# Two chained transformer layers on one core: the end of the expert stage and the start of the second block are re-ordered

## The chip, the cores and the metric

The kernel runs on one core of a Trainium2 chip. The metric is the device time of one execution in microseconds (us), the median of several runs; less is better. TensorE (PE) multiplies matrices, VectorE (DVE) and ScalarE (ACT) do elementwise work, GpSimd (POOL) issues the indirect gathers, SyncE (SP) issues the other transfers.

## The reference

Two blocks are chained, on 512 tokens of width 1024. What matters here is the seam between them:

```
# end of block 1
f = peer_ffn(hn2, ...)              # expert mixture: sum over picked experts of gelu(h.u[e]) * gate * v[e]
x = x + gate2 * f
x = rmsnorm(x, final_g)             # output of block 1
# start of block 2
h  = concat([16 meta tokens, x])    # 528 rows
n1 = rmsnorm(h, norm1_w)
q, k, v, fg, u = split(n1 @ w_in)   # k is normed per head
mix = concat([forgetting_attention(q, k, v, cumsum(log_sigmoid(fg))), pooled_means(u) @ w_pool]) @ w_out
h = h + mix                         # then a gated feed-forward layer; the meta rows are dropped at the end
```

## The kernel before, in words

Activations lie transposed (width on the partitions), 128 tokens to a tile, four tiles. A float32 product is made of three PE passes over a high and a low part (`mm3`, L189 to L191). Weights come by DMA as float32 chunks (`raw`), and `split_chunk` (L176 to L185) makes of each the pair `whi` (an ACT copy, L183) and `wlo` (a DVE subtraction, L184). Both parts lie in rings of a few slots that are taken in turn (`ring`, L107 to L117); a chunk's slot is that of the chunk some places earlier, so its copy waits until the last matmul on that earlier chunk is done. While `open_raw` is in force the ring has extra slots behind the base ones.

Each engine works through its own list of instructions in order. The order of a list is set when the program is built, by a scheduler that weighs the written order, its own costs for each instruction and readiness; `issue_after` ties an instruction behind another.

*Expert stage.* Three of the four token tiles ("dense" tiles) are multiplied with all expert rows: 128 chunks, each a 128x1024 slice of `v`, accumulate in six PSUM banks `a`, two for each tile. The fourth tile (`GB`) instead gathers its picked rows one by one (POOL indirect DMA into `grow`, DVE L1056 adds each into `gacc`). `GFUSE` and `GTAIL` set how many gathers are written beside each chunk and how many chunks before the end the last one stands. The last three chunks (`VT`) are written apart, tile by tile.

*Finisher* (`fin`, L1165 to L1187), once for each tile: z = f times gate2 (L1169 for GB, L1174 for a dense tile, in two halves read from PSUM), x += z (L1170 or L1175), a row sum of squares on ACT (L283), x *= final_g (L1177), a second row sum, two reciprocal roots by small 128x1 operations (L267 to L275; their root on ACT), the norm rows z = x * r2 * w1 (L1184), PE transposes and a split of these into `nh`, `nl` (L249, L256, L257), and x *= r1 (L1186, the output of block 1 itself). `z` has one of two slots `fz`. `meta_norm` (L1189) does the 16 meta rows.

*Key stage.* `k2_proj` (L1201) splits the four key weight chunks, then `go` projects the keys of a tile in two halves of the width (`part` 0 and 1), and `headnorm` norms them per head (`hq`, `hss`, `ks`). `KORD` is the order: small letters are first halves, capitals second halves (m meta, g GB, a, b, c the dense tiles), f the finisher of the last dense tile. Then come the q projection (`q_fill`), the forget gate features (PE into a 72-row tile, added on DVE at L1301), values, and eight attention heads with other work filled between them (`B2F`).

*End of block 2's mixing.* `mix_fill` (L1420) multiplies the pooled half of the width with its part of `w_out`, and adds to x in L1431, on 128x512. The attention half is `gemm_rows` on `w_out` (L1479) in four chunks, whose ring has extra slots from `open_raw` at L1460, after the attention pool is closed.

Of the kernel before, what the change touches and what calls it, by code (L numbers as in the profile page):

```python
# [11 lines left out]
F32 = mybir.dt.float32  # L12
F32R = mybir.dt.float32r
# [11 lines left out]
D = 1024  # L25
KC = 8
# [25 lines left out]
LAG = 6  # L52
CB = 4
GBB = 2
GFUSE = 2.75
GTAIL = 6
GLAG = 3
NGAT = 257 + GLAG
VT = 3
# [6 lines left out]
WPF = ('', '', 'a', '', 'ra', 'ra', 'ra', 'r')  # L66
ADKB = 3
TG = 4
KORD = 'amfbgcMAGBC'
B2F = ('', 'b', 'af', 'q', 'ec', 'dg', 'vijkh', 'lCAB', 'DW', 'XY', 'Z')  # L70
CANDS = ((0, 1, 16, 0), (1, 4, 8, 16), (4, 8, 4, 40), (8, 16, 1, 56))
GSC = 16384.0
# [3 lines left out]
class Kern:  # L76
# [73 lines left out]
    def consts(self):  # L150
        nc, I, cp = self.nc, self.I, self.cp
        self.table()
        cst = cp.tile([128, 5, 128], F32, name="cst")
        nc.sync.dma_start(cst, I["cst"].rearrange("c p n -> p c n"))
        self.ident = cst[:, 0]
        self.cneg = cst[:, 3]
        self.identb = cp.tile([128, 128], BF, name="identb")
        nc.vector.tensor_copy(self.identb, cst[:, 0])
        self.ntri = cp.tile([128, 128], F32R, name="ntri")
        nc.vector.tensor_copy(self.ntri, cst[:, 1])  # L160
        self.nones = cp.tile([128, 128], F32R, name="nones")
        nc.vector.memset(self.nones.bitcast(F32), -1.0)
        self.onesf = cp.tile([128, 128], F32, name="onesf")
        nc.vector.memset(self.onesf, 1.0)
        self.strictT = cp.tile([128, 128], BF, name="strictT")
        nc.vector.tensor_copy(self.strictT, cst[:, 2])
        self.cposb = cp.tile([128, 128], BF, name="cposb")
        nc.vector.tensor_scalar(self.cposb, cst[:, 3], -1.0, None, op0=ALU.mult)
        self.iota = cst[:, 4]
        self.epsc = cp.tile([128, 1], F32, name="epsc")  # L170
        nc.vector.memset(self.epsc, EPS)
        self.cols2 = cp.tile([128, 6], F32, name="cols2")
        self.iota_h = cp.tile([128, 128], HF, name="iota_h")
        nc.vector.tensor_copy(self.iota_h, cst[:, 4])

    def split_chunk(self, src):  # L176
        nc = self.nc
        shp = [128] + list(src.shape[1:])
        raw = self.row(shp)
        self.loaded = nc.sync.dma_start(raw, src).ins  # L180
        hi = self.ring(shp, F32R, "whi")
        lo = self.ring(shp, F32R, "wlo")
        nc.scalar.activation(hi, raw, AF.Copy)  # L183
        self.lastlo = nc.vector.tensor_tensor(lo, raw, hi, op=ALU.subtract).ins  # L184
        return hi, lo  # L185
# [74 lines left out]
            r = nc.vector.scalar_tensor_tensor(lo, src, scale, hi, op0=ALU.mult, op1=ALU.subtract)  # L260
        return r.ins

    def rstd(self, pool, ssum, n, cols, rows=128, eps=None):
        nc = self.nc
        h, r, q = [pool.tile([128, cols], F32, name=self.nm("r" + c))[:rows] for c in "hrq"]
        e, eh = (self.epsc[:, 0:1], -0.5 * EPS) if eps is None else eps
        nc.vector.tensor_scalar(h, ssum, -0.5 / n, eh, op0=ALU.mult, op1=ALU.add)  # L267
        nc.scalar.activation(r, ssum, AF.Ln, scale=1.0 / n, bias=e[:rows])
        nc.scalar.activation(r, r, AF.Exp, scale=-0.5)
        if cols == 1:  # L270
            nc.vector.scalar_tensor_tensor(q, h, r, r, op0=ALU.mult, op1=ALU.mult)
        else:
            nc.vector.tensor_tensor(q, r, r, op=ALU.mult)
            nc.vector.tensor_tensor(q, q, h, op=ALU.mult)
        nc.vector.scalar_tensor_tensor(r, q, 1.5, r, op0=ALU.add, op1=ALU.mult)  # L275
        return r

    def sumsq(self, pool, src, n, rows=128):
        nc = self.nc
# [715 lines left out]
    def peer(self):  # L995
# [138 lines left out]
        self.ks = pa.tile([128, 2, 4, W1], F32R, name="ks")  # L1134
        kctx = ExitStack()
        pn = kctx.enter_context(tc.tile_pool(name="b2k", bufs=1))
        tgen = self.v_chunk(pv, accs, tail)
        next(tgen)
        kproj = self.k2_proj(pn)
        fin(dense[0], accs[0])  # L1140
        fin(dense[next(tgen)], accs[1])
        next(tgen)
        for c in KORD:
            if c == "f":
                fin(dense[2], accs[2])
            else:
                t = (-1, GB, *dense)["mgabcMGABC".index(c) % 5]
                kproj((t,), "mgabcMGABC".index(c) // 5)
# [5 lines left out]
    def finisher(self, pool):  # L1154
        nc, I = self.nc, self.I
        self.table()
        rows = {}
        for k, src in (("g2", self.modrow[3:4]), ("fg", I["final_g"]), ("w1", I["n1w"])):
            rows[k] = self.grows()
            with self.tc.issue_after(self.loaded):  # L1160
                self.brow(rows[k], src)
        self.n1w = rows["w1"]
        self.n1 = n1h, n1l = self.act_pair(W1)

        def fin(t, f):  # L1165
            x = self.x[:, t]
            z = pool.tile([128, D], F32, tag="fz", bufs=2, name=self.nm("fz"))
            if t == GB:
                nc.vector.tensor_tensor(z, f, rows["g2"], op=ALU.mult)  # L1169
                nc.vector.tensor_tensor(x, x, z, op=ALU.add)  # L1170
            else:
                for n in range(2):
                    c = ts(n, 512)
                    nc.vector.tensor_tensor(z[:, c], f[n], rows["g2"][:, c], op=ALU.mult)  # L1174
                    nc.vector.tensor_tensor(x[:, c], x[:, c], z[:, c], op=ALU.add)  # L1175
            s1 = self.sumsq(pool, x.unsqueeze(1), 1)
            nc.vector.tensor_tensor(x, x, rows["fg"], op=ALU.mult)  # L1177
            s2 = self.sumsq(pool, x.unsqueeze(1), 1)
            r1 = self.rstd(pool, s1, D, 1)
            e2 = pool.tile([128, 2], F32, name=self.nm("e2"))  # L1180
            nc.vector.tensor_scalar(e2[:, 0:1], s1, EPS / D, EPS * EPS, op0=ALU.mult, op1=ALU.add)
            nc.vector.tensor_scalar(e2[:, 1:2], s1, -0.5 * EPS / D, -0.5 * EPS * EPS, op0=ALU.mult, op1=ALU.add)
            r2 = self.rstd(pool, s2, D, 1, eps=(e2[:, 0:1], e2[:, 1:2]))
            nc.vector.scalar_tensor_tensor(z, x, r2, rows["w1"], op0=ALU.mult, op1=ALU.mult)  # L1184
            self.rows_out(n1h, n1l, META + 128 * t, z, None if t == GB else self.psa)
            nc.vector.tensor_scalar(x, x, r1, None, op0=ALU.mult)  # L1186
        return fin  # L1187

    def meta_norm(self, pool):  # L1189
        nc = self.nc  # L1190
        n1h, n1l = self.n1
        mt = pool.tile([128, D], F32, tag="fz", bufs=2, name="mt")[:META]
        nc.sync.dma_start(mt, self.I["meta"])
        rm = self.rstd(pool, self.sumsq(pool, mt.unsqueeze(1), 1, META), D, 1, META)
        nc.vector.scalar_tensor_tensor(mt, mt, rm, self.n1w[:META], op0=ALU.mult, op1=ALU.mult)
        p = self.psg()
        for k in range(KC):
            nc.tensor.transpose(p[:, ts(k, META)], mt[:, ts(k, 128)], self.ident[:META, :META])
        self.hilo(n1h[:, :, 0:META], n1l[:, :, 0:META], p[:, 0:KC * META].rearrange("p (k n) -> p k n", n=META))

    def k2_proj(self, pn):  # L1201
        tc, I = self.tc, self.I
        n1h, n1l = self.n1
        wv = I["w_in_2"].rearrange("(k p) n -> p k n", p=128)
        kwc = self.cols2[:, 1:2]
        ck = [self.split_chunk(wv[:, kc:kc + 2, 512:1024]) for kc in range(0, KC, 2)]

        ps = {}

        def go(ts_, part):  # L1210
            for t in ts_:
                c = slice(0, META) if t < 0 else slice(META + 128 * t, META + 128 * t + 128)
                m = META if t < 0 else 128
                if part != 1:
                    p = ps[t] = self.psg() if t in (-1, GB) else self.psa()
                    for k in range(KC):
                        hi, lo = ck[k // 2]
                        self.mm3(p[:m], n1h[:, k, c], n1l[:, k, c], hi[:, k % 2], lo[:, k % 2], k == 0, k == KC - 1)
                if part != 0:
                    self.headnorm(pn, ps[t], kwc, self.ks, c, m)  # L1220
        return go

    def headnorm(self, pool, p, wcol, dst, off, rows, half=None, q=None, ps=None):
        nc = self.nc
# [25 lines left out]
    def block2(self, out):  # L1250
# [170 lines left out]
        def mix_fill(g):  # L1421
            hi, lo = self.split_chunk(wov[:, 4:8, ts(g, 256)])
            for tp in (0, 2):
                p = self.psg()
                for k in range(4):
                    mh_, ml_ = mixed(4 + k)
                    for t in range(2):
                        c = ts(tp + t, 128)
                        self.mm3(p[:, ts(t, 256)], mh_[:, c], ml_[:, c], hi[:, k], lo[:, k], k == 0 and t == 0, k == 3, skip=True)
                xs = x[:, tp:tp + 2, ts(g, 256)]  # L1430
                nc.vector.tensor_tensor(xs, xs, p.rearrange("p (t n) -> p t n", n=256), op=ALU.add)  # L1431

        fill = {"q": lambda: q_fill(1), "v": lambda: v_fill(1)}
        for g in range(4):
# [182 lines left out]
```

## Time and profile before

| quantity | value |
|---|---|
| median of three runs | 2385.33 us (2384.72 to 2385.57) |
| profiled execution | 2384.28 us, span of its trace 2382.4 us |
| PE busy | 2302.8 us, 97% of the span |
| DVE, ACT, POOL busy | 73%, 43%, 14% |
| last expert matmul starts | 1752.36 us from the start of the span |

The time axis of every view starts at the start of the span. A row of the timeline is one instruction, or several alike in a row; the bracket at its end is the time that the engine had been idle before it, and who released it. PE rows overlap, since a matmul starts before the one ahead of it has drained: the distance between two starts is what one costs.

### The profile page before, as it was taken

Reading aid. Unit: us, or ns where it says so; the run is one execution under the profiler, and the core shown is the slowest. Engines: PE = TensorE matmul, PEld = TensorE weight load, DVE = VectorE, ACT = ScalarE, POOL = GpSimd, SP = SyncE. Lnnn points to the kernel's source line nnn. Section 1 sums busy time; section 2 is a strip of 40 time slices with the busy share of each in tenths; the row PEclk is TensorE's granted clock in tenths of the full one; section 3 lists DMA queues with packets and bytes.
Section 4 is the critical chain, followed back from the end, with each engine's and each line's share of the span. In section 5 each row is a group of like instructions: output and inputs, shape, how many; then the busy total and the mean of one; then the engine's idle time right before and its main releaser. Section 6 shows DMA issues by size and latency. Waiting matters only on the chain.

```text
span 2382.4 us, 33726 instructions
## 1 busy us (share of the span) xinstructions
PE 2302.8 (97%) x12405; PEld 2013.1 (85%) x12409; DVE 1744.0 (73%) x3421; ACT 1030.3 (43%) x1642; POOL 326.3 (14%) x286
## 2 busy tenths in 40 slices
PE   7999888999999999999999999999989989999999
PEld 6888766778899999999999988888868878888887
DVE  7689876677998998876888898888886765333321
ACT  3587444243355665553333333333345543322211
POOL 0000000000000323432344432222200000000000
PEclk9999999999999999999999999999989989999999
DMA  9432644652255999989999999999943312333231
GB/s 268 116 98 63 187 141 132 207 165 80 87 179 165 349 357 352 340 337 331 313 334 340 339 376 358 334 338 348 343 136 91 102 36 80 107 97 97 90 116 43
DMA packets 282217, 498.63 MB, mean 209 GB/s; under 512 B 19442, under 2 KB 176754, under 8 KB 280516
## 3 DMA queue, kind: packets, MB, share of 16 engines
q1 hardware_dynamic: 243268, 355.96, 44.8%
q0 software_dynamic: 38784, 140.53, 16.9%
q8 instruction: 97, 1.59, 0.3%
q14 instruction: 68, 0.56, 0.1%
HBM read 444.98 MB, written 47.76 MB: 207 GB/s over the span
## 4 chain that ended last, share of the span: by engine, by line
PE 91%; DVE 5%; ACT 1%; issue 1%; DMA 1%; SPq 0%; DVEq 0%; ACTq 0%
PE a L190 17%; PE a L189 17%; PE a L191 17%; PE g L189 11%; PE g L190 11%; PE g L191 10%; PE g L962 2%; PE a L421 1%; DVE wlo L184 1%; PE g L421 1%; PE g L422 1%; PE a L675 0%; PE a L422 0%; PE a L674 0%; DVE nl L257 0%
## 5 line engine op out<-in xcount | busy, mean ns | idle before, releaser
L183 ACT ACTIVATE whi<-raw 128x1024 fp32r<-128x1024 f32 x425 | 446.5, 1054 | 682.6 <-PE g L190 343.8
L184 DVE TENSOR_TENSOR wlo<-raw,whi 128x1024 fp32r<-128x1024 f32 x425 | 518.2, 1221 | 297.9 <-ACT whi L183 288.1
L189 PE MATMUL g<-nh,whi 128*128 128x512 f32 (+4 forms) x1024 | 384.2, 375 | 10.8 <-DVE ya L460 7.8
L190 PE MATMUL g<-nl,whi 128*128 128x512 f32 (+4 forms) x1024 | 383.3, 374 | 0.0
L191 PE MATMUL g<-nh,wlo 128*128 128x512 f32 (+4 forms) x1024 | 381.4, 372 | 0.0
L190 PE MATMUL a<-nl,whi 128*128 128x384 f32 (+2 forms) x912 | 309.8, 340 | 1.3 <-DVE nl L257 1.2
L189 PE MATMUL a<-nh,whi 128*128 128x384 f32 (+2 forms) x912 | 303.7, 340 | 3.4 <-ACT nh L256 3.3
L191 PE MATMUL a<-nh,wlo 128*128 128x384 f32 (+2 forms) x912 | 305.2, 335 | 0.4 <-DVE wlo L184 0.4
L190 PE MATMUL a<-wlo,ch 128*128 128x512 f32 x768 | 298.6, 389 | 0.0
L191 PE MATMUL a<-whi,cl 128*128 128x512 f32 x768 | 297.9, 389 | 0.0
L189 PE MATMUL a<-whi,ch 128*128 128x512 f32 x768 | 264.0, 389 | 0.0
L1038 POOL DMA_INDIRECT grow<-in_u_dram,eidx x128 | 152.4, 1191 | 764.2 <-DVE o_g L941 433.1
L189 PEld LDWEIGHTS g<-nh,whi 128*128 128x128 f32 (+1 forms) x1024 | 193.0, 188 | 42.3 <-DVE ya L460 8.4
L191 PEld LDWEIGHTS g<-nh,wlo 128*128 128x128 f32 (+1 forms) x1024 | 193.3, 189 | 29.5 <-issue 0.2
L190 PEld LDWEIGHTS g<-nl,whi 128*128 128x128 f32 (+1 forms) x1024 | 193.0, 188 | 29.5
L256 ACT ACTIVATE ch<-cf 128x384 fp32r<-128x384 f32 x128 | 67.1, 525 | 319.3 <-issue 182.9
L1038 POOL DMA_INDIRECT grow<-in_v_dram,eidx x128 | 159.4, 1246 | 318.4 <-DVE gacc L1056 269.7
L189 PEld LDWEIGHTS a<-nh,whi 128*128 128x128 f32 x912 | 173.6, 191 | 6.4 <-ACT nh L256 4.1
L190 PEld LDWEIGHTS a<-nl,whi 128*128 128x128 f32 x912 | 173.4, 190 | 4.6 <-DVE nl L257 2.0
L191 PEld LDWEIGHTS a<-nh,wlo 128*128 128x128 f32 x912 | 174.1, 191 | 2.9 <-DVE wlo L184 0.8
L191 PEld LDWEIGHTS a<-whi,cl 128*128 128x128 f32 x768 | 144.2, 188 | 29.8
L190 PEld LDWEIGHTS a<-wlo,ch 128*128 128x128 f32 x768 | 144.1, 188 | 28.9
(398 smaller groups left out, 3947.6 us busy)
## 6 DMA issues: line engine op xcount, KB each, us to landing
raw<-in_u_t_dram SPq DMA_DIRECT2D x128, 512.0 KB
raw<-in_v_dram SPq DMA_DIRECT2D x128, 512.0 KB
raw<-in_w_in_dram SPq DMA_DIRECT2D x54, 512.0 KB
gdr<-gblk SPq DMA_DIRECT2D x12, 2048.0 KB
vg<-gdr SPq DMA_DIRECT2D x192, 128.0 KB
udr<-ug SPq DMA_DIRECT2D x44, 384.0 KB
vu<-udr SPq DMA_DIRECT2D x44, 384.0 KB
adaraw<-in_w_ada_dram SPq DMA_DIRECT2D x32, 512.0 KB
```

Of the source, the lines that this page charges most:

```text
L183: nc.scalar.activation(hi, raw, AF.Copy)
L184: self.lastlo = nc.vector.tensor_tensor(lo, raw, hi, op=ALU.subtract).ins
L189: mm(out, lhsT=lh, rhs=rh, start=start, stop=False, skip_group_check=skip)
L190: mm(out, lhsT=lh, rhs=rl, start=False, stop=False, skip_group_check=skip)
L191: mm(out, lhsT=ll, rhs=rh, start=False, stop=stop, skip_group_check=skip)
L256: nc.scalar.activation(hi, src, AF.Copy)
L421: mm(out, lhsT=st, rhs=mh, start=start, stop=False, skip_group_check=skip)
L422: mm(out, lhsT=st, rhs=ml, start=False, stop=stop, skip_group_check=skip)
L962: nc.tensor.matmul(p[:, ts(j, 128)], lhsT=s2[:, c], rhs=rep[k][:, c // 2, :, c % 2], start=(i == 0), stop=(i == 1))
L1038: nc.gpsimd.indirect_dma_start(out=u, out_offset=None, in_=I[src], in_offset=bass.IndirectOffsetOnAxis(ap=eidx[:, i:i + 1], axis=0))
```

## The change

The four key weight chunks are no longer split in one go inside `k2_proj`. It hands out a function that splits the next ones: the first is taken from the ring ahead of the last three expert chunks, the second goes to a tile of its own in the pool `b2k` (`split_chunk` has a `pool` argument), the third and fourth follow in the ring, one of them written behind the latest x += z (`self.added`). The norm rows of GB overwrite its accumulator `gacc`, those of the last dense tile get a tile of their own in `b2k`, and the meta rows use a `grow` slot. The order of key tiles `KORD` changes, and so do `GFUSE` and `GTAIL`. The multiplication x *= r1 at the end of the finisher is dropped: r1 is kept in `xr`, one column for each tile, and the additions of `mix_fill` become x = x * xr + p, one instruction for each token tile (128x256) instead of one for two (128x512).

```
-GFUSE = 2.75
-GTAIL = 6
+GFUSE = 2.95
+GTAIL = 10
-KORD = 'amfbgcMAGBC'
+KORD = 'gamfGMbcABC'
+        self.xr = cp.tile([128, TB], F32, name="xr")
-    def split_chunk(self, src):
+    def split_chunk(self, src, pool=None):
...
-        hi = self.ring(shp, F32R, "whi")
-        lo = self.ring(shp, F32R, "wlo")
+        hi, lo = [self.ring(shp, F32R, k) if pool is None else pool.tile(shp, F32R, name=self.nm(k)) for k in ("whi", "wlo")]
...
-        nc.vector.scalar_tensor_tensor(r, q, 1.5, r, op0=ALU.add, op1=ALU.mult)
-        return r
+        out = r if out is None else out
+        nc.vector.scalar_tensor_tensor(out, q, 1.5, r, op0=ALU.add, op1=ALU.mult)
+        return out
...
         pn = kctx.enter_context(tc.tile_pool(name="b2k", bufs=1))
+        kw, kproj = self.k2_proj(pn)
+        kw(1)
+        kw(1, pn)
         tgen = self.v_chunk(pv, accs, tail)
         next(tgen)
-        kproj = self.k2_proj(pn)
         fin(dense[0], accs[0])
+        with tc.issue_after(self.added):
+            kw(2)
         fin(dense[next(tgen)], accs[1])
         next(tgen)
...
-                fin(dense[2], accs[2])
+                fin(dense[2], accs[2], pn)
...
-        def fin(t, f):
+        def fin(t, f, zp=None):
-            z = pool.tile([128, D], F32, tag="fz", bufs=2, name=self.nm("fz"))
+            z = f if t == GB else (zp or pool).tile([128, D], F32, tag="fz", bufs=1 if zp else 2, name=self.nm("fz"))
...
-                    nc.vector.tensor_tensor(x[:, c], x[:, c], z[:, c], op=ALU.add)
+                    self.added = nc.vector.tensor_tensor(x[:, c], x[:, c], z[:, c], op=ALU.add).ins
...
-            r1 = self.rstd(pool, s1, D, 1)
+            self.rstd(pool, s1, D, 1, out=self.xr[:, t:t + 1])
...
-            nc.vector.tensor_scalar(x, x, r1, None, op0=ALU.mult)
-        mt = pool.tile([128, D], F32, tag="fz", bufs=2, name="mt")[:META]
+        mt = self.grows()[:META]
-        ck = [self.split_chunk(wv[:, kc:kc + 2, 512:1024]) for kc in range(0, KC, 2)]
+        ck = []
+        def weights(n, pool=None):
+            for _ in range(n):
+                kc = 2 * len(ck)
+                ck.append(self.split_chunk(wv[:, kc:kc + 2, 512:1024], pool))
...
-                xs = x[:, tp:tp + 2, ts(g, 256)]
-                nc.vector.tensor_tensor(xs, xs, p.rearrange("p (t n) -> p t n", n=256), op=ALU.add)
+                for t in (tp, tp + 1):
+                    xs = x[:, t, ts(g, 256)]
+                    nc.vector.scalar_tensor_tensor(xs, xs, self.xr[:, t:t + 1], p[:, ts(t - tp, 256)], op0=ALU.mult, op1=ALU.add)
```

The lists of POOL are the same in both programs, and those of PE, DVE and ACT are the same up to the last chunks of the expert stage. In the changed program the finisher's lines stand five lower (L1174 is gacc times gate2, L1175 x += gacc, L1179 and L1180 the two steps of a dense tile, L1182 x *= final_g, L1189 the norm rows). Three places follow.

On DVE, from GB's x += z to the first norm rows, before (`fz_16960` is GB's z, the three `wlo` are key weights; small 128x1 operations are left out at "..."):

```order
L1170 TENSOR_TENSOR x<-x,fz_16960 128x1024
L184 TENSOR_TENSOR wlo_17183<-raw_17180,whi_17182 128x1024
L1177 TENSOR_TENSOR x<-x,grow_16954 128x1024
...
L184 TENSOR_TENSOR wlo_17189<-raw_17186,whi_17188 128x1024
L184 TENSOR_TENSOR wlo_17195<-raw_17192,whi_17194 128x1024
...
L1184 SCALAR_TENSOR_TENSOR fz_16960<-x,rr_16982,grow_16956 128x1024
```

And now (`a_11310` to `a_11315` are the six expert banks, `fz_17185` and `fz_17261` the z of two dense tiles, `wlo_17638` belongs to the forget gate's weights):

```order
L1175 TENSOR_TENSOR x<-x,gacc 128x1024
L1179 TENSOR_TENSOR fz_17185<-a_11310,grow_16816 128x512
L1179 TENSOR_TENSOR fz_17185<-a_11311,grow_16816 128x512
L1182 TENSOR_TENSOR x<-x,grow_16818 128x1024
...
L1180 TENSOR_TENSOR x<-x,fz_17185 128x512
L1179 TENSOR_TENSOR fz_17261<-a_11312,grow_16816 128x512
...
L184 TENSOR_TENSOR wlo_17240<-raw_17237,whi_17239 128x1024
...
L184 TENSOR_TENSOR wlo_17638<-raw_17635,whi_17637 128x576
...
L184 TENSOR_TENSOR wlo_17715<-raw_17712,whi_17714 128x1024
...
L1182 TENSOR_TENSOR x<-x,grow_16818 128x1024
...
L1189 SCALAR_TENSOR_TENSOR gacc<-x,rr_16845,grow_16820 128x1024
```

The reads of all six expert banks, their additions, one dense tile's x *= final_g and three `wlo` now stand ahead of the first norm rows; the first of them is placed ahead of GB's own x *= final_g.

On PE, at the end of the q projection's first half (matmuls into `a_17714`, `a_17715`), where the last key tiles' `hq` are transposed, before:

```order
L191 MATMUL a_17714<-whi_17772,nl_16959 128x256
L189 MATMUL a_17715<-whi_17772,nh_16958 128x256
L1244 MATMUL g_17583<-cst,hq_17569 128x128 x4
L190 MATMUL a_17715<-wlo_17773,nh_16958 128x256
L191 MATMUL a_17715<-whi_17772,nl_16959 128x256
L1244 MATMUL g_17606<-cst,hq_17592 128x128 x4
L189 MATMUL a_17715<-whi_17772,nh_16958 128x256
```

And now (`g_17633` is the forget gate feature):

```order
L190 MATMUL a_17711<-wlo_17769,nh_16822 128x256
L191 MATMUL a_17711<-whi_17768,nl_16823 128x256
L1253 MATMUL g_17556<-cst,hq_17542 128x128 x4
L1253 MATMUL g_17579<-cst,hq_17565 128x128 x4
L1253 MATMUL g_17602<-cst,hq_17588 128x128 x4
L189 MATMUL g_17633<-nh_16822,whi_17637 72x264
```

The transposes of three key tiles stand together behind the last matmul of the projection; before, those of two tiles stood among its matmuls. On ACT the last tile's `hq_17588` now stands behind the copies of the next two weight chunks (`whi_17885`, `whi_17951`):

```order
L183 ACTIVATE whi_17885<-raw_17883 128x1024
L259 ACTIVATE ks<-g_17483,cols_168 64x4x16
L268 ACTIVATE rr_17570<-hss_17567,epsc_166 128x8
L269 ACTIVATE rr_17570<-rr_17570 128x8
L183 ACTIVATE whi_17951<-raw_17949 128x1024
L259 ACTIVATE ks<-g_17556,cols_168 64x4x128
L1236 ACTIVATE hq_17588<-a_17517 128x512
```

On ACT at the end of the eighth head: the copies of the four `w_out` chunks before (`whi_19643`, `whi_19649` are chunks 0 and 1; `whi_19655`, `whi_19661` are 2 and 3; `g_19614` is the last head's output):

```order
L183 ACTIVATE whi_19643<-raw_19641 128x1024
L183 ACTIVATE whi_19649<-raw_19647 128x1024
L455 ACTIVATE y_17633<-g_19510 64x512
...
L455 ACTIVATE y_17633<-g_19614 64x512
L458 ACTIVATE osum_19625<-g_19614 64x512
L256 ACTIVATE nh_19005<-y_17633 128x512
L183 ACTIVATE whi_19655<-raw_19653 128x1024
L183 ACTIVATE whi_19661<-raw_19659 128x1024
```

And now (`whi_19647`, `whi_19653` are chunks 0 and 1, `whi_19659`, `whi_19665` are 2 and 3, `g_19618` the last head's output):

```order
L183 ACTIVATE whi_19659<-raw_19657 128x1024
L183 ACTIVATE whi_19665<-raw_19663 128x1024
...
L456 ACTIVATE y_17629<-g_19618 64x512
L459 ACTIVATE osum_19629<-g_19618 64x512
L256 ACTIVATE nh_19001<-y_17629 128x512
L183 ACTIVATE whi_19647<-raw_19645 128x1024
L183 ACTIVATE whi_19653<-raw_19651 128x1024
```

With one ring take fewer in the key stage the four chunks fall on other slots: chunks 2 and 3 are now copied before the last head ends, and chunks 0 and 1, with which the accumulation starts on PE, after it.

## Rows read from the trace of the kernel before

**Rows 1.** The page, section 4: shares of the span in the chain that ended last.

```profile
PE 91%; DVE 5%; ACT 1%; issue 1%; DMA 1%; SPq 0%; DVEq 0%; ACTq 0%
```

**Rows 2.** What PE waited for, 1725 to 1835 us: total, times, longest (us).

```profile
PE g L249 <- DVE fz L1184: 6.0, 1, 6.0
PE a L249 <- DVE fz L1184: 4.3, 1, 4.3
PE g L191 <- DVE nl L257: 1.5, 1, 1.5
PE g L189 <- DVE ks L260: 0.8, 1, 0.8
```

**Rows 3.** Timeline of PE: the last expert matmul, and the key stream's steady start.

```profile
1752.36 0.39 PE L191 MATMUL a<-whi,cl 128*128 128x512 f32 x1
...
1765.75 0.61 PE L191 MATMUL g<-whi,nl 128*16 128x512 f32 x1 [1.49 <-DVE nl L257]
```

**Rows 4.** Windows: busy us (instructions) of PE, PEld, DVE, ACT, POOL; granted clock; DMA.

```profile
1765.00:1770.00 5.00, 4.25 (x11) 1.42 (x11) 3.79 (x11) 3.55 (x8) 0.00 (x0) 0.50 0.01 3
1770.00:1775.00 5.00, 5.00 (x22) 2.97 (x21) 4.37 (x12) 3.68 (x12) 0.00 (x0) 0.95 0.00 0
...
1790.00:1795.00 5.00, 3.95 (x15) 3.54 (x16) 4.63 (x10) 1.20 (x2) 0.00 (x0) 0.66 0.00 0
```

**Rows 5.** DVE by line and form, 1744 to 1830 us: busy us, mean ns, idle before.

```profile
L184 DVE TENSOR_TENSOR wlo<-raw,whi 128x1024 fp32r<-128x1024 f32 x8 | 9.7, 1223 | 6.6 <-ACT whi L183 6.6
L260 DVE SCALAR_TENSOR_TENSOR ks<-g,cols,ks 64x512 fp32r<-64x512 f32 x8 | 5.8, 748 | 0.3
L1184 DVE SCALAR_TENSOR_TENSOR fz<-x,rr,grow 128x1024 f32<-128x1024 f32 x4 | 5.1, 1273 | 0.0
L1177 DVE TENSOR_TENSOR x<-x,grow 128x1024 f32<-128x1024 f32 x4 | 4.9, 1219 | 1.5 <-ACT junk L283 1.5
...
L1175 DVE TENSOR_TENSOR x<-x,fz 128x512 f32<-128x512 f32 x6 | 4.0, 674 | 0.0
L1174 DVE TENSOR_TENSOR fz<-a,grow 128x512 f32<-128x512 f32 x6 | 3.8, 676 | 1.2 <-PE a L249 1.2
L1186 DVE TENSOR_SCALAR x<-x,rr 128x1024 f32<-128x1024 f32 x4 | 3.0, 746 | 0.0
...
L1231 DVE TENSOR_TENSOR hq<-a,rr 128x512 f32<-128x512 f32 x3 | 2.0, 689 | 0.1
...
L275 DVE SCALAR_TENSOR_TENSOR rr<-rq,rr 128x1 f32<-128x1 f32 x8 | 1.2, 155 | 0.1
L184 DVE TENSOR_TENSOR wlo<-raw,whi 128x576 fp32r<-128x576 f32 x1 | 0.8, 759 | 6.7 <-ACT whi L183 6.7
```

**Rows 6.** Timeline of DVE behind the first norm rows.

```profile
1759.44 1.27 DVE L1195 SCALAR_TENSOR_TENSOR mt<-mt,rr,grow 16x1024 f32<-16x1024 f32 x1
...
1761.23 1.27 DVE L1174 TENSOR_TENSOR fz<-a,grow 128x512 f32<-128x512 f32 x2
1762.43 0.67 DVE L257 TENSOR_TENSOR nl<-g,nh 128x512 fp32r<-128x512 f32 x1
```

**Rows 7.** Timeline of ACT at the end of the expert stage.

```profile
1750.07 1.06 ACT L183 ACTIVATE whi<-raw 128x1024 fp32r<-128x1024 f32 x1 [8.41 <-PE a L191]
```

**Rows 8.** Timeline of ACT behind the last attention head.

```profile
1985.88 0.59 ACT L455 ACTIVATE y<-g 64x512 f32<-64x512 f32 x1 [9.53 <-PE g L450]
...
1987.84 0.63 ACT L256 ACTIVATE nh<-y 128x512 fp32r<-128x512 f32 x1 [0.76 <-DVE y L460]
1988.37 1.99 ACT L183 ACTIVATE whi<-raw 128x1024 fp32r<-128x1024 f32 x2
```

**Rows 9.** Window of the same place, columns as in rows 4.

```profile
1980.00:1990.00 10.00, 10.00 (x60) 8.64 (x59) 3.31 (x5) 3.35 (x5) 0.00 (x0) 1.00 0.11 30
```

**Rows 10.** The whole span by line and form: the mixing additions, and a PE group.

```profile
L189 PE MATMUL g<-whi,nh 128*128 128x256 f32 x288 | 82.9, 289 | 1.2 <-DVE x L1431 0.8 <-DVE pmx L257 0.4
...
L1431 DVE TENSOR_TENSOR x<-x,g 128x512 f32<-128x512 f32 x8 | 5.5, 688 | 16.1 <-PE g L191 16.1
```

More of the change, by code (lines that the diff above doesn't have):

```diff
@@ L261, in hilo, with rstd @@
         return r.ins
-    def rstd(self, pool, ssum, n, cols, rows=128, eps=None):
+    def rstd(self, pool, ssum, n, cols, rows=128, eps=None, out=None):
         nc = self.nc
@@ L1220, in go @@
                     self.headnorm(pn, ps[t], kwc, self.ks, c, m)
-        return go
+        return weights, go
     def headnorm(self, pool, p, wcol, dst, off, rows, half=None, q=None, ps=None):
```

## Prediction, made before the changed kernel ran

> **What bounds the kernel now.** First the chain of waits: 91% of the span is PE's own work [rows 1], so an edit counts only where PE stands still or runs slowly. Then PE's waits around the seam: four large ones, 6.0, 4.3, 1.5 and 0.8 us [rows 2]. The last expert matmul starts at 1752.36 and lasts 0.39 [rows 3]; call its end, 1752.75, T. The first key transposes wait until T+6.0 for GB's norm rows, and matmuls flow without a break only from 1765.75 on; the two ahead of it take 0.43 each (11 in 4.25 us, with a granted clock of 0.50 [rows 4]), so the stream began, in effect, at 1764.9, which is T+12.1. [...] After the 4.3 us wait the window has a mean of 0.66: 3.4 us at half speed, 1.7 lost [rows 4]. The waits of rows 2 end with a DVE instruction, so next I read DVE [rows 5, 6], and, as ACT feeds it, ACT [rows 7].
>
> At T DVE is late because ACT was: a key weight copy held ACT for 8.41 us for a ring slot [rows 7], and GB's row sum of squares stood behind it. That is what the change takes away. The question is what takes its place.
>
> **Term A, the first norm rows.** In the changed list DVE must do, from the first read of an expert bank to the norm rows: six reads L1179 and six additions L1180, at 0.60 each (a pair starting at 1761.23 lets the next start at 1762.43 [rows 6]; additions have the same length, 674 ns against 676 [rows 5]): 7.2 us. Two x *= final_g at 1.22 less the overlap of neighbours (0.08: two of 0.676 take 1.27, [rows 5, 6]), 1.14 each: 2.3. Two `wlo` of 1.22 and one of 0.76, with that overlap 3.0 [rows 5]. Sixteen small column operations at about 0.08 (155 ns less overlap [rows 5]): 1.3. Sum 13.8 us. The start is fixed from the other side: the first read waits for bank `a_11310`, whose last matmul stands eleventh from the end, so it is ready ten matmuls, at 5.0/22 = 0.23 us [rows 4], ahead of T: T-2.3. GB's x *= final_g stands behind that read although its row sum is long done. So the norm rows start at T+11.5 and, at 1.27 [rows 5], end at T+12.8, against T+6.0: PE's first wait is 12.8. Behind them DVE has the meta rows (1.27 [rows 6]), another x *= final_g (1.14), some 0.5 of small ones and two `nl` of 0.60 pitch, 4.1 in all, so key matmuls start at about T+17.0. Against T+12.1: **+4.9**. Bounds: +4.0 if the small operations cost nothing and reads and banks overlap better, +6.5 if ACT's root operations come late between them.
>
> The half speed behind it: the stream now starts four us after the transposes, so the clock can be back earlier. Bounds 1.5 to 2.8 lost against 2.8; I take 1.9: **-0.9**.
>
> **Term B, the second wait.** The 4.3 us for the last tile's norm rows go: their three L1189 end by T+24, at a pitch of about 3 us behind the first, and PE needs them some twenty us later. With them go the 1.7 of half speed: **-6.0**. Nothing is late next there; key weights 2 and 3 are split while PE does 18 q matmuls.
>
> **Term C, a new wait at the end of the first q projection.** The order on PE puts the transposes of three key tiles in one row behind the projection's last matmul, and the features behind them. The last tile's `hq` is copied on ACT behind `whi_17951`, whose slot is the one that this very projection reads to its last matmul. So from that matmul on a chain runs with PE empty: weight copy 1.0 [rows 8], `wlo` 1.22, four `ks` products at 0.75, a sum and a scaling of 128x512 at 0.69, some 0.4 of small ones [rows 5]: 7.0, less eight overlaps of 0.08 is 6.4, less 0.5 in which PE does the first two tiles' transposes: 5.9. The 0.8 of rows 2 is in it. Half speed behind it, by the same measure as after the 4.3 wait, 0 to 1.7; I take 1.0 as the features are short. **+5.9 - 0.8 + 1.0 = +6.1**. Bounds: +3 if half of the chain were to start earlier, +7.
>
> **Term D, `w_out`.** Chunks 0 and 1 open the accumulation, and their copies now stand behind the last head's output. In the profile PE had no idle time there [rows 9], since chunks 0 and 1 were ready and PE filled with them. The same chain of ACT can be read: output copy at 1985.88, high part at 1987.84, first weight copy from 1988.37, two in 1.99, so the first ends at 1989.4 [rows 8]. That is 3.6 us without work for PE, and then half speed as after 4.3 us, 1.7: **+5.3**. Bounds: 0, if the scheduler's other fill covers it, to 6.4 with the second copy waited for too.
>
> **What costs nothing.** The four x *= r1 (0.75 each [rows 5]) stood behind norm rows that PE waits for, or beside PE's matmuls: 0, at most -0.7 where the first one delayed the meta rows. Eight mixing additions of 0.69 become sixteen of half the columns; PE waited 0.8 us for them in all [rows 10]. Bounds for one: 0.16 (the small operations of rows 5) to 0.69, so that a pair takes between 0.3 and 1.4, and the eight between -3 and +5.6 on DVE; PE's work lies over it, and I take 0. Gathers: POOL's list is the same, and the last gathered rows are added on DVE ahead of the same two or three weight chunks as before, so `GFUSE` and `GTAIL` move nothing here: 0.
>
> [...]
>
> **Sum.** +4.9 - 0.9 - 6.0 + 6.1 + 5.3 = +9.4. The durations are of one profiled execution of 2384.28 us (span 2382.4 and 1.9 around it), which lies 1.05 under the median of the runs; the difference is added to the median: 2385.33 + 9.4 = 2394.7 us.
>
> **Rivals.** *The seam gains as the edit reads.* If DVE's list let GB's rows go first, ACT's early freedom would move them 3.1 us ahead (row sum at 1748 after the last addition, and not behind the weight copy of rows 7), and with term B, and C and D covered, 3.1 + 6.0 = -9.1: 2376.2. For it: both waits that it aims at are in the trace. Against it: a queue that hands on only its head. The trace shows that ACT did not pass over its blocked copy for 8.41 us [rows 7]. [...] It decides if the first norm rows start before T+4.8.
>
> *Only the seam loses, or only `w_out`.* If D is covered, 2385.3 + 4.1 = 2389.4; if C is covered, 2385.3 - 2.0 + 5.3 = 2388.6. For it: fills are placed by costs that I read only as an order. Against: both orders show the late instruction directly in front of what PE needs. 0.17.
>
> *Dearer on every term,* with A at +6.5, C at +7, D at +6.4 and the mixing additions at +1.3 on PE: -0.9 - 6.0 + 21.2 = +14.3, 2399.6. For it: half speed may last longer than after 4.3 us when waits come close together. Against: bounds rarely fall together. 0.10.
>
> *The change does not do what it says:* with GB's sums ready ahead of T and no weight copy blocked, but the same picks at the same place. That is in the sum already.
>
> **How the numbers follow.** The forecast has 0.66, between 2391 and 2398. The bound for no change is 0.2%, 4.8 us, about what a measurement of this kernel can tell: 2380.6 to 2390.1. Slower: forecast and dear case, 0.76; same: the case with one term covered, 0.17; faster: 0.07. The range goes from 2386.5, below the single-term cases, to 2400.5, above the dear one; outside stay the fast rival and the ends of the others.
>
> **What would show it.** In the changed profile: PE's first wait on L249 near 12.8 us, released by the norm rows L1189 (right), or under 6 (A wrong). No wait on L249 near T+38 (B). A wait of about 6 us on L1253 near T+67 with ACT's L183 and DVE's L184 in its chain (C). An idle PE of 3 to 4 us after the last head, ended by ACT L183, with a granted clock near 0.66 behind it (D). The prediction is wrong if the sum of PE's waits from T to T+72 is below the 12.6 of [rows 2], or if PE stays at 10.00 of 10 through the last head.

## The result, and the profile after

The changed kernel takes 2400.39 us (median of 4 runs, 2397.95 to 2402.43) against 2385.43: the ratio is 1.0062, 95% interval 1.0049 to 1.0075, 15.0 us slower. Forecast were 9.4 us, 2394.7, in a range of 2386.5 to 2400.5, with a chance of 0.66 for 2391 to 2398.

These are the waits of PE in the changed kernel from 1700 us on (total, times, longest), to be read against [rows 2]:

```profile
PE g L249 <- DVE gacc L1189: 12.9, 1, 12.9
PE g L1253 <- DVE hq L1240: 7.0, 1, 7.0
...
PE a L189 <- ACT whi L183: 3.6, 1, 3.6
...
PE g L1202 <- DVE nl L257: 1.4, 1, 1.4
```

The wait of 4.3 us on the last tile's rows is gone, the first one has doubled, and two new ones stand there. PE's timeline shows where. T is again the end of the last expert matmul, here 1753.07, 0.3 later than before:

```profile
1752.68 0.39 PE L191 MATMUL a<-whi,cl 128*128 128x512 f32 x1
1765.92 1.97 PE L249 MATMUL g<-cst,gacc 128*128 128x128 f32 x8 [12.86 <-DVE gacc L1189]
...
1770.25 0.80 PE L189 MATMUL g<-whi,nh 128*128 128x512 f32 x1
...
1822.74 1.09 PE L1253 MATMUL g<-cst,hq 128*128 128x128 f32 x4 [7.00 <-DVE hq L1240]
1823.48 0.57 PE L189 MATMUL g<-nh,whi 128*72 128x264 f32 x1
...
1989.96 0.79 PE L189 MATMUL a<-whi,nh 128*128 128x512 f32 x1 [3.62 <-ACT whi L183]
```

This is DVE in the first of these waits, to be read against [rows 5, 6]. Reads of the banks, additions and weight splits fill it without a gap, and the norm rows come at the end.

```profile
1750.84 1.29 DVE L1179 TENSOR_TENSOR fz<-a,grow 128x512 f32<-128x512 f32 x2 [1.98 <-PE a L191]
1752.04 1.22 DVE L1182 TENSOR_TENSOR x<-x,grow 128x1024 f32<-128x1024 f32 x1
...
1756.36 1.21 DVE L184 TENSOR_TENSOR wlo<-raw,whi 128x1024 fp32r<-128x1024 f32 x1
...
1760.82 1.22 DVE L184 TENSOR_TENSOR wlo<-raw,whi 128x1024 fp32r<-128x1024 f32 x1
...
1762.68 1.21 DVE L1182 TENSOR_TENSOR x<-x,grow 128x1024 f32<-128x1024 f32 x1
...
1764.60 1.27 DVE L1189 SCALAR_TENSOR_TENSOR gacc<-x,rr,grow 128x1024 f32<-128x1024 f32 x1
```

ACT stands as follows at the two new waits, to be read against [rows 8]. At the end of the q projection (PE's last matmul of it starts at 1814.58) come a weight copy and then `hq`; behind the last head come the output copy and then the first chunks of `w_out`.

```profile
1814.90 1.06 ACT L183 ACTIVATE whi<-raw 128x1024 fp32r<-128x1024 f32 x1 [3.71 <-PE a L191]
...
1816.57 0.58 ACT L1236 ACTIVATE hq<-a 128x512 f32<-128x512 f32 x1
...
1986.37 0.59 ACT L456 ACTIVATE y<-g 64x512 f32<-64x512 f32 x1 [6.46 <-PE g L451]
...
1988.87 1.99 ACT L183 ACTIVATE whi<-raw 128x1024 fp32r<-128x1024 f32 x2
```

DVE goes on with the chain of the first of these two, and each instruction starts only when the one before it has ended:

```profile
1815.99 1.23 DVE L184 TENSOR_TENSOR wlo<-raw,whi 128x1024 fp32r<-128x1024 f32 x1 [2.12 <-ACT whi L183]
1817.25 0.74 DVE L260 SCALAR_TENSOR_TENSOR ks<-g,cols,ks 64x512 fp32r<-64x512 f32 x1
1818.02 0.69 DVE L1238 TENSOR_REDUCE hss<-hq 128x8 f32<-128x512 f32 x1
...
1821.90 0.69 DVE L1240 TENSOR_TENSOR hq<-a,rr 128x512 f32<-128x512 f32 x1
```

The next windows (columns as in rows 4) show half speed (a granted clock of 0.50, or a mean between that and 1.00) behind each of the three waits, and last a window of the last matmul stage, to which the prediction did not look.

```profile
1770.00:1775.00 5.00, 5.00 (x18) 4.00 (x18) 4.88 (x16) 3.22 (x10) 0.00 (x0) 0.62 0.01 3
...
1820.00:1825.00 5.00, 2.26 (x11) 2.29 (x12) 3.00 (x8) 0.89 (x2) 1.06 (x2) 0.50 0.07 25
1825.00:1830.00 5.00, 5.00 (x31) 5.00 (x29) 1.56 (x3) 0.68 (x1) 0.35 (x1) 0.66 0.00 0
...
1990.00:1995.00 5.00, 5.00 (x12) 3.93 (x13) 2.30 (x2) 0.85 (x1) 0.00 (x0) 0.50 1.10 295
...
2300.00:2320.00 20.00, 20.00 (x87) 16.09 (x87) 4.90 (x4) 3.33 (x4) 0.00 (x0) 1.00 0.25 85
```

The same stretch before, where PE does 90 matmuls in 20 us at the same granted clock:

```profile
2300.00:2320.00 20.00, 20.00 (x90) 16.54 (x89) 6.50 (x8) 4.24 (x4) 0.00 (x0) 1.00 0.37 131
```

Between the two traces PE falls back by 0.3 us up to T, by 6.5 from there to the last forget gate feature (L1301 starts at 1824.9 before, L1310 at 1831.8 after), by 4.8 from there to the gate stage of the feed-forward layer (first matmul 2036.3 and 2047.9), by 0.5 in it, and by 3.5 in the last stage (130.6 and 134.1 us long); 1.1 more lies behind the last matmul. These add up to 16.7, the difference of the two profiled spans; the medians are 15.0 apart.

### The profile page after: what moved, and what is told of

It reads as the page before. It is cut to its first block, busy times and chain, and to the rows that moved or that the text cites. A ratio compares the mean times of both kernels' runs of the same rounds, so it can differ in the third digit from the quotient of the medians.

```text
span 2399.1 us, 33729 instructions
## 1 busy us (share of the span) xinstructions
PE 2308.9 (96%) x12409; PEld 2016.8 (84%) x12409; DVE 1743.6 (73%) x3425; ACT 1029.9 (43%) x1642; POOL 320.8 (13%) x286
## 4 chain that ended last, share of the span: by engine, by line
PE 90%; DVE 6%; DMA 1%; ACT 1%; issue 1%; SPq 0%; DVEq 0%; ACTq 0%
PE a L189 18%; PE a L190 17%; PE a L191 17%; PE g L189 10%; PE g L191 10%; PE g L190 10%; PE g L963 2%; DVE wlo L184 1%; DVE iacc L308 1%; DVE ptl L257 0%; PE a L422 0%; DMA adaraw<-in_w_ada_dram 0%; PE g L422 0%; PE a L676 0%; PE g L423 0%
## 5 line engine op out<-in xcount | busy, mean ns | idle before, releaser
L1039 POOL DMA_INDIRECT grow<-in_v_dram,eidx x128 | 153.8, 1201 | 324.2 <-DVE gacc L1057 275.6
L189 PEld LDWEIGHTS a<-nh,whi 128*128 128x128 f32 x912 | 174.0, 191 | 5.9 <-ACT nh L256 3.6
```

The costliest lines, as they stand in the source:

```text
L189: mm(out, lhsT=lh, rhs=rh, start=start, stop=False, skip_group_check=skip)
L1039: nc.gpsimd.indirect_dma_start(out=u, out_offset=None, in_=I[src], in_offset=bass.IndirectOffsetOnAxis(ap=eidx[:, i:i + 1], axis=0))
```

## The experiments

The theories are that the loss is the sum of the late norm rows (A), the chain at the end of the q projection (C) and the late `w_out` chunks (D), less the wait that is gone (B); and, for the last stage, that the place of the tiles in memory sets its pace. The rivals are that a wait is only moved, or that the last stage's pace is a matter of the run. A "before" of its own ran beside each group of four: 2384.82, 2385.24, 2385.19. The ratios are to these. The changed kernel's own median is known to about 3 us (interval 1.0049 to 1.0075), so where a run is set against it, the trace has to bear the reading out.

**e1.** The column tile made wider, so that later tiles stand 64 bytes higher, not 32.

```
-        self.xr = cp.tile([128, TB], F32, name="xr")
+        self.xr = cp.tile([128, 4 * TB], F32, name="xr")
```

> The changed kernel with xr made four times as wide (64 bytes for each partition instead of 16, which take 32). Nothing else differs, and the order on each engine is the same. In the changed program all tiles behind the constants lie 32 bytes higher than before; with this padding they lie 64 bytes higher. Theory (place of the tiles): the last matmul stage runs at 0.227 us for each 512-column matmul before and at 0.233 after because the stationary tiles acth and actl moved by 32 bytes against the moving weights, so here it is 0.227 again and the time is 3.5 to 4.5 us below the changed kernel, about 2396. Rival (the pitch is a matter of the run, or of what ran before the stage): 0.233 stays or varies, and the time stays at 2400 within the spread of the changed kernel's runs.

2402.43 us, ratio 1.0077 (1.0063 to 1.0091); 87 matmuls from 2300 to 2320. 64 bytes do not bring the pace back.

**e2.** The kernel before with a tile of 16 bytes that nothing reads.

```
         self.cols2 = cp.tile([128, 6], F32, name="cols2")
+        self.xr = cp.tile([128, TB], F32, name="xr")
```

> The kernel before with a constant tile of 16 bytes for each partition (32 with rounding) that nothing reads. The order on each engine is as before. Theory (place of the tiles): the last stage goes from 0.227 to 0.233 us for each matmul, and the time rises by 3.5 to 4.5 us to about 2389.5. Rival: no change, 2385.4 within 1.

2388.38 us, ratio 1.0016 (1.0007 to 1.0025): 3.6 us for a tile that nothing uses, with the last stage at the slower pace:

```profile
2300.00:2320.00 20.00, 20.00 (x88) 16.09 (x87) 4.95 (x5) 3.90 (x4) 0.00 (x0) 1.00 0.24 81
```

So the place of the tiles is a cause; e1 shows only that 64 bytes do not bring the pace back.

**e3.** The ring index set back where the extra slots open.

```
         self.ext = {"raw": n - RAW0, "whi": wb - W0, "wlo": wb - W0}
+        for k in ("whi", "wlo"):
+            if self.ri.get(k, 0) >= W0:
+                self.ri[k] = 0
```

> The changed kernel with one addition: where the ring gets its extra slots, its index starts again at the first base slot. So chunks 0 and 1 of w_out fall on base slots again. Theory (term D): PE's wait of 3.6 us for the weight copy behind the last head goes, with the half speed behind it, 1.7: 5 us less than the changed kernel, about 2395. Rival (the wait only moves to the next chunk or the time is lost again in the norm behind it): 2399 to 2400.

2394.26 us, ratio 1.0038 (1.0024 to 1.0051), 6 under the changed kernel. PE is full behind the last head, so D is a term of its own. Between the traces it is worth 5.7 us, near the 5.3 forecast (from the last feature to the gate stage 210.4 us, in the changed kernel 216.1):

```profile
1985.00:1995.00 10.00, 10.00 (x56) 8.51 (x55) 5.12 (x8) 3.83 (x5) 0.00 (x0) 1.00 0.13 40
```

**e4.** The reads of the expert banks tied behind GB's norm rows.

```
-                    nc.vector.tensor_tensor(z[:, c], f[n], rows["g2"][:, c], op=ALU.mult)
+                    with self.tc.issue_after(self.gbrows):
+                        nc.vector.tensor_tensor(z[:, c], f[n], rows["g2"][:, c], op=ALU.mult)
...
-            nc.vector.scalar_tensor_tensor(z, x, r2, rows["w1"], op0=ALU.mult, op1=ALU.mult)
+            zi = nc.vector.scalar_tensor_tensor(z, x, r2, rows["w1"], op0=ALU.mult, op1=ALU.mult).ins
+            if t == GB:
+                self.gbrows = zi
```

> The changed kernel with the six reads of the expert banks (L1179) tied behind GB's norm rows on DVE. Theory (term A: the place in DVE's list alone makes the first wait long): PE's first wait falls from 12.9 us to below 4. What that is worth: the split of GB's rows and the meta rows still stand behind the six reads and the additions, so a wait of about 12 us comes right behind the first transposes, the key matmuls start at about T+17 as in the changed kernel, and the time stays within 2 us of 2400. Rival (the first wait is the price): the time falls by 6 to 9 us to 2391 to 2394.

2401.3 us, ratio 1.007 (1.0057 to 1.0084). The first wait is 2.2 and the next 12.6:

```profile
1752.99 1.71 PE L249 MATMUL g<-cst,gacc 128*128 128x128 f32 x8 [2.23 <-DVE gacc L1190]
1767.31 1.00 PE L1205 MATMUL g<-cst,grow 16*128 16x16 f32 x8 [12.61 <-DVE xr L276]
```

The list's order alone made the first wait, as A says; but its price is what DVE has to do before key matmuls can start, and that only changed places. They start at 1768.24, 17.5 us behind the end of the last expert matmul (1750.76 in this trace), as in the changed kernel (17.2).

**e5.** As e1 with 128 bytes (`8 * TB`).

> The changed kernel with xr made eight times as wide, 128 bytes for each partition, so that every tile behind the constants stands 128 bytes higher than before. The shift of 64 bytes left the last stage at 0.233 us for each matmul. Theory (place modulo 128 bytes: the stage is at 0.227 when the stationary tiles stand at the same byte as the moving weights, modulo 128; all weight slots and the expert stage's ch and cl stand at 96, acth and actl at 96 before, at 0 in the changed kernel, at 32 with 64 bytes more): 0.227 comes back and the time is 3.5 us under the changed kernel, 2396 to 2397.5. Rival (any shift of the tiles costs, or something else in the changed program does): 0.233, 2400 to 2402.

2401.06 us, ratio 1.0067 (1.0053 to 1.0081), 88 matmuls in the window. The theory in this form, modulo 128 bytes, fell.

**e6.** Three slots for `hq`.

```
-            q = pool.tile([128, 512], F32, tag="hq", bufs=2, name=self.nm("hq"))[:rows]
+            q = pool.tile([128, 512], F32, tag="hq", bufs=3, name=self.nm("hq"))[:rows]
```

> The changed kernel with three slots for hq in place of two, in the key stage and in the q projection. Theory (term C: the third key tile's hq waits for the transposes of the first, which stand behind the projection's last matmul, and a chain of 7.0 us runs with PE empty): the wait on L1253 goes, the forget gate feature starts 4 to 5 us earlier, and another wait of 2 to 4 us for a PSUM bank comes in its place; in all 2 to 4 us less than the changed kernel, about 2397.5. Rival (the ring slot of the weight copy alone holds it): the wait stays at 7, no change.

2396.76 us, ratio 1.0042 (1.0028 to 1.0055), 3.6 under the changed kernel; the intervals of the two overlap, but the traces agree with 3.1 (from T to the last feature 75.6 and 78.7 us). The wait of 7.0 goes and one of 3.9 comes:

```profile
PE g L249 <- DVE gacc L1189: 12.9, 1, 12.9
PE g L189 <- DVE ks L260: 3.9, 1, 3.9
```

With the third slot the scheduler also put `hq` ahead of the two weight copies on ACT, so the slot and the place in ACT's list are not told apart.

**e7.** Before with the last tile's own tile and the new `KORD` alone.

```
-KORD = 'amfbgcMAGBC'
+KORD = 'gamfGMbcABC'
...
-                fin(dense[2], accs[2])
+                fin(dense[2], accs[2], pn)
...
-            z = pool.tile([128, D], F32, tag="fz", bufs=2, name=self.nm("fz"))
+            z = (zp or pool).tile([128, D], F32, tag="fz", bufs=1 if zp else 2, name=self.nm("fz"))
```

> The kernel before with two parts of the change alone: the last dense tile's norm rows get a tile of their own, and the order of the key tiles is the new one. Weight splits, gathers, GB's rows, the meta rows' place and the additions are as before; no tile behind the constants moves. Theory (term B is worth having by itself; A, C, D and the place of the tiles came with the other parts): the wait of 4.3 us on L249 falls to about 1, the first wait rises from 6.0 to about 7.5, no new wait at the end of the q projection and none behind the last head: 6 to 8 us under the kernel before, 2377 to 2379. Rival (without the early weight split the gain is lost on DVE): within 2 us of 2385.

2377.93 us, ratio 0.9965 (0.9953 to 0.9977): 7.3 us faster than before. The tile and the order are not told apart by it. Its waits around the seam:

```profile
PE g L249 <- DVE fz L1184: 7.8, 1, 7.8
PE g L189 <- DVE nl L257: 0.8, 1, 0.8
PE a L249 <- DVE fz L1184: 0.7, 1, 0.7
```

**e8.** Before with `GFUSE` and `GTAIL` alone.

> The kernel before with GFUSE 2.95 and GTAIL 10 alone. Theory (POOL's list stays, and the last gathered rows are bound by the gathers themselves): no change, 2384 to 2386, PE's first wait 6.0. Rival (picks end earlier and ACT with them): the first wait falls by 1 us or more and the time with it.

2384.7 us, ratio 0.9997 (0.9988 to 1.0006), PE's first wait 6.0: no change.

**e9.** As e1 with 256 bytes (`16 * TB`).

> The changed kernel with xr made 256 bytes wide for each partition, so that every tile behind the constants stands 256 bytes higher than before. Shifts of 32, 64 and 128 bytes all left the last stage at 0.233 us for each matmul. In the traces so far the pitch of 512-column matmuls goes with one number: the place of the stationary tile less that of the moving one, modulo 256 bytes; at 0 it is 0.227, elsewhere 0.230 to 0.234. Theory: with 256 bytes the last stage is at 0.227 again and the time is 3 to 4 us under the changed kernel, about 2397. Rival (the place does not decide): 0.233, 2400 to 2402.

2396.73 us, ratio 1.0049 (1.0035 to 1.0063), 3.7 under the changed kernel. Here too the intervals overlap, but the trace has the last stage at 130.6 us, 3.5 under the changed kernel's, with 90 matmuls in the window:

```profile
2300.00:2320.00 20.00, 20.00 (x90) 16.57 (x89) 3.85 (x4) 3.57 (x4) 0.00 (x0) 1.00 0.31 106
```

**e10.** e3, e6 and e9 together.

> The changed kernel with three cures at once: three slots for hq (alone worth 3.6 us), the ring index started again at the extra slots (alone 6), xr of 256 bytes (if the place decides, 3.5). Theory (the loss is the sum of separate terms, and what is left is term A less term B): 2400.4 - 13.1, about 2387, with PE's first wait still 12.9 and none on L249 later. Rival (the terms overlap): 2390 to 2394.

2389.14 us, ratio 1.0016 (1.0007 to 1.0025, which is 1.7 to 6.0 us above before). Taking the three single gains off the changed kernel gives 2387.0, at the low end of that interval; the rival's 2390 lies within it too, so the run doesn't settle whether the cures add up in full. Of PE's waits around the seam these are left:

```profile
PE g L252 <- DVE gacc L1192: 12.8, 1, 12.8
PE g L192 <- DVE ks L263: 3.9, 1, 3.9
PE g L1205 <- DVE nl L260: 1.4, 1, 1.4
```

**e11.** Before with the scaled mixing additions alone: r1 is copied to `xr`, which is 256 bytes wide here, so that no tile moves modulo 256.

> The kernel before with one part of the change: x *= r1 is left out of the finisher, r1 is kept in xr (here 256 bytes wide, so that no tile moves modulo 256) and used in the mixing additions, sixteen of 128x256 for eight of 128x512. Theory (the additions lie beside PE's work, the dropped products too): within 1.5 us of before, 2384 to 2386.5, an addition at about 0.48. Rival (the smaller additions come through to PE): 1 to 3 us more than before.

2386.6 us, ratio 1.0005 (0.9996 to 1.0015): not told apart from no change, nor from the rival's 1 to 3 us. An addition takes 0.477:

```profile
L1433 DVE SCALAR_TENSOR_TENSOR x<-x,xr,g 128x256 f32<-128x256 f32 x16 | 7.0, 477 | 12.1 <-PE g L192 12.1
```

**e12.** e7 with the activation tiles seen in rows of 2048 bytes.

```
-        return tuple(self.ap.tile([128, KC, W1], F32R, tag=k, name=self.nm(k))[:, :, 0:w] for k in ("nh", "nl"))
+        return tuple(self.ap.tile([128, KC * W1], F32R, tag=k, name=self.nm(k))[:, 0:KC * w].rearrange("p (k n) -> p k n", n=w) for k in ("nh", "nl"))
```

> The kernel of e7 with the activation tiles nh and nl seen as rows of 512 columns (2048 bytes) where 512 are used, in place of rows of 528 (2112 bytes) of which 512 are used. The memory, the order on each engine and the arithmetic are those of e7. Counted in the program, pairs of a long matmul and the next weights with places equal modulo 256 bytes rise from 4301 to 8238 of about 8960. Theory (place modulo 256 decides the pitch): the projections of block 1 and the gate and up stage go from 0.232 to 0.227 us for 512 columns, some 1600 of these at 5.5 ns and some 2240 of 384 columns at about as much: 15 to 22 us under e7, 2356 to 2363. Rival (only the stationary tile's place, or the last stage, is sensitive): 2376 to 2379.

2370.15 us, ratio 0.9932 (0.9918 to 0.9945): 15 us faster than before and the fastest of all, but 7.8 under e7 where 15 to 22 were expected. The gate stage came to the expected pace, 88 matmuls in e7 and 90 here:

```profile
2080.00:2100.00 20.00, 20.00 (x88) 16.23 (x87) 7.29 (x8) 6.42 (x8) 0.00 (x0) 1.00 0.30 86
```

```profile
2080.00:2100.00 20.00, 20.00 (x90) 16.57 (x89) 7.30 (x8) 6.39 (x8) 0.00 (x0) 1.00 0.35 103
```

It is 4.5 us shorter (211.3 and 206.8 from its first matmul to the last stage), and the expert stage starts 5.0 earlier. What was over-sized are the 384-column matmuls: their mean distance went from 0.176 to 0.174, not by 5.5 ns; and 1.4 us were lost again between the expert stage and the gate stage.

## Why the prediction was right, and where it was short

The mechanism was forecast in its three places, with the right releasers, and the kernel is slower for these reasons. That the time lies in the range is in part luck: it is 0.1 us inside the upper end and above the 2391 to 2398 that had most of the weight, and 3.5 of the 15.0 us come from a term that isn't in the sum. Without these it would be about 2396.9; e9, which takes them away, has 2396.7.

- **Term A: right.** First wait 12.9 for 12.8; the norm rows run at T+11.5 as summed; key matmuls start at 1770.25, T+17.2 for T+17.0. Half speed lasted to 1773.8 (mean clock 0.62 in 1770 to 1775), 1.8 lost for 1.9. The 2.8 that the sum sets against it can be read in the trace before. The granted clock, which has two values in both traces, 0.50 and 1.00, is 0.50 there from 1756.9 to 1770.5, and long key matmuls start 0.43 us apart until then, 0.23 apart behind it; from 1764.9 on this is 5.6 us, of which half is lost. One reading in the prediction is off without weight: the 0.43 us of a half-speed matmul is ten distances in 4.25 us, where eleven would give 0.39.
- **Term B: right.** There is no wait on L249 for the last tile, and e7 gains 7.3 us with its tile and the new key order alone, although its first wait rises from 6.0 to 7.8.
- **Term C: the right place and chain, a size too small.** 7.0 for 5.9. Some 0.6 of the 1.1 are the eight overlaps of 0.08 that were subtracted and didn't come: a `wlo` of 1.23 us starts at 1815.99 and the next product at 1817.25. And the features ran at half speed to 1828.4 (0.50, then 0.66), 4.9 us, 2.4 lost where 1.0 was taken "as the features are short". Together A, B and C come to 17.2 - 12.1 - 1.0 - 6.0 + 7.0 - 0.8 + 2.4 = +6.7, the 6.5 of the traces within 0.2, for +4.1 forecast.
- **Term D: right wait, half speed too short.** 3.6 for 3.6, but PE's granted clock was 0.50 from 1989.96 to 1995.6, 2.8 lost for 1.7. That is 6.4 for 5.3, while the traces are only 4.8 apart from the last feature to the gate stage, so 1.6 us came back on the way. In e3, which has no D, 1.0 of it is there too (210.4 us, 211.4 before), and what gives that back is not shown. For the rest PE's waits at the transposes behind the mixing (L249) account, 3.9 us before and in e3 and 3.0 in the changed kernel.
- **A term that was missing: the place of the tiles.** The prediction gave the column tile `xr` no price. Its 32 bytes moved `acth` and `actl` against the weight slots, and the last stage went from 0.227 to 0.233 for each of 528 matmuls, 3.5 us. e2 shows it without any other part of the change (3.6), e9 takes it away from the changed kernel (3.7). No row of the trace before priced it, but one could have put the question: the expert stage and the last stage ran at 0.227 and the gate stage at 0.232, at the same granted clock of 1.00.
- **The rivals.** The fast one is out: its condition, norm rows before T+4.8, isn't met, and e4, which meets it (norm rows at 1751.65, T+0.9), gains nothing. So that sign could not have told the fast case from the forecast: the key matmuls also need the meta rows and the splits, which DVE does later. DVE didn't pass over a blocked instruction either: in the changed kernel GB's x *= final_g was ready at 1750.05, when ACT's row sum had ended, and DVE stood idle until 1750.84, when the first bank read, ahead of it in the list, could start. The case with one term covered is out too, since both C and D came. The dear one, 2399.6, is near in time, yet not by its mechanism: A stayed at its forecast and for the mixing additions PE waits 1.1 us, 0.8 before. No run shows the +1.3 that it has for these: in the changed kernel one takes 0.476 us and the sixteen 7.0 of DVE, where the eight took 5.5 [rows 10]. Whether the additions cost anything e11 leaves open.
- **Picks:** 0 was forecast, and e8 shows nothing that can be told from 0.

What is left in e10 over before is 1.7 to 6.0 us by the medians and 3.5 between the traces from T to the gate stage, 3.3 of it ahead of the last feature. There stand the longer first wait and the 3.9 us that took the place of 7.0, less term B; no run takes these apart.

## What to carry to other kernels

When work is pulled ahead of a wait, list everything that now stands in front of the instruction that the bottleneck waits for, on its engine: here 13.8 us of DVE's work, ready in time and placed too early. A ring take fewer or more moves the phase of every later stage; look which chunk opens the next accumulation. A new small tile can cost time by shifting the others, as the 16 bytes that nothing reads cost 3.6 us in e2: compare the pace of long matmul stages before and after.

## What the runs showed of the hardware that was not expected

In these traces the pace of a long stage of 512-column float32 matmuls goes with the places of their operands in memory. These are read from the programs, not from a profile. The number that it goes with is the place of the stationary tile less that of the moving one, modulo 256 bytes. Where it is 0 for every pair, a matmul starts 0.227 us after the one before it; with other values, 0.231 to 0.235, all at a granted clock of 1.00 or close to it. In the trace before, 0 has a mean of 227.3 ns (some 3390 pairs, distances of 0.26 us and more left out; 2830 of them in the expert stage and the last stage, where every pair has 0) and the other values together 232.6 (some 2160). It does not decide a single pair: in the gate stage before, where 0 is mixed with 64, 128 and 192, the pairs with 0 have 230.2 and the others 232.2 to 232.7, and in e12, where all have 0, they have 227.4 (90 in a window of 20 us, 88 before). With 384 columns it is weaker: 174.8 ns at 0, 174.0 at 128 and 178.7 at 64 before. In the last stage:

| kernel | difference modulo 256 | us per matmul | against the changed kernel |
|---|---|---|---|
| before, e7, e11, e12 | 0 | 0.2267 | |
| changed, e2 | 32 | 0.2333 | |
| e1 | 64 | 0.2333 | +2.0 us |
| e5 | 128 | 0.2333 | +0.7 us |
| e9 | 0 (moved by 256) | 0.2267 | -3.7 us |

The differences of time of e1 and e5 are within the spread of the runs. Why 256, and what collides, no run here shows.
